# Layer-1 retention in a two-layer hybrid backbone: token tiles copied by ScalarE ahead of the first scores, and VectorE in program order up to them

## The chip, the cores and the metric

The kernel runs on one core of a Trainium2 chip. The engines of a core run their own instruction streams and wait for each other through semaphores: TensorE (PE, matmuls, reads SBUF and writes the PSUM banks), VectorE (DVE), ScalarE (ACT), GpSimd (POOL), and SyncE (SP), which here only issues transfers. The metric is device time in microseconds of one execution, the median of three runs.

## The reference

Two layers over 256 latent tokens and 256 context tokens of width 1024. Layer 0 is windowed attention beside a gated linear recurrence. Layer 1, the last, is a retention mixer, and each layer ends with a SwiGLU network. The part that matters here is the start of layer 1 (cut, names kept):

```python
def modulate(h, shift, scale):
    return h * (1.0 + scale) + shift

h_lat = modulate(rms_norm(x, norm_g[layer, 0]), m_lat[0], m_lat[1])
h_ctx = modulate(rms_norm(ctx, norm_g[layer, 0]), m_ctx[0], m_ctx[1])

def odd_mixer(h_ctx, h_lat, w_in, w_out, cos, sin, need_ctx):   # 4 heads, dk 256, dv 512
    p = split_parts(h_lat @ w_in, ODD_PARTS)                      # q, k, v, gate
    pc = project_parts(h_ctx, w_in, ODD_PARTS, ['k', 'v'])        # last layer: context gives k, v only
    q_l = apply_rope(q of p); k_l = apply_rope(k of p) * k_scale
    # forward and backward retention: scores (q k^T) times a decay matrix, times v, over latent and context
    y_lat = gated_head_norm(o_fw + flip(o_bw), p['g']).astype(dt) @ w_out
```

## The kernel before, in words

**Precision.** Every fp32 operand of a large matmul is split into two parts of type fp32r: a high half, which ScalarE makes by a rounding copy, and a rest (value minus high half), which VectorE makes. A product is three matmuls: high x high, rest x high, high x rest (L341, L342, L343; L338 and L339 do it in two where the operand's parts lie side by side). Tiles `hh` and `hl` are high half and rest of the normed input, `whi` and `wlo` those of a weight piece, `u` are working tiles.

**Weights.** All weights stream in one sequence of pieces of 128 x 1024. `ensure` loads a piece into one of three `raw` buffers (SP issues the transfer), ScalarE makes `whi` (L268), VectorE `wlo` (L269), each with four buffers. A raw buffer is free for the next transfer when its `wlo` is made; a `whi` buffer when TensorE has read it.

**Order.** The kernel is written against a scheduler that chooses each engine's instruction order from the dependences; inside `tc.manual_schedule` an engine keeps the order in which the program calls it. Side work is written as generators in lanes ('b', 'c', 't', 'r'). `work` counts matmul columns and now and then takes one step of each lane; `drain(lane)` runs a lane to its end. `modt` sets how many such steps lie between two rows of the modulation matrix (L233).

**Start of layer 1.** The norm of the latent stream runs ahead of its statistics: `first_group` multiplies the unnormed, scaled latent input (258 columns: 256 tokens and the shift) and afterwards `fix` (L458, L459) scales the four results by the norm's factor. For the context stream, and for the latent input of the later groups, `Norm.finish` works block by block (eight blocks of 128 rows): `scaled` (L478, VectorE) puts the scaled block into a tile, `shifted` makes its high half with the shift added (L484, ScalarE) and its rest (L485, VectorE). Lane 'b' holds the latent stream's finish, lane 'c' the context's. After the group comes the context's part of the keys (`pc`), then:

- `rope` (L1071 to L1073) rotates keys and query on VectorE, and `split` (L435 on ScalarE, L436 on VectorE) makes their halves;
- `tok_lane` multiplies the normed input by an identity (L1086, L1087), which lays it out by tokens: four token blocks times two halves of the width, eight tiles in PSUM, each split into `htok`;
- `ret_gate` projects the gate (two column blocks), `ret_scores` makes the scores (two banks of 128 x 512), multiplies them by the decay matrix (L1143) and splits them;
- `ret_values` sums the token tiles with the scores (`sums`), and projects the sums with the value weights (L338, L339), eight steps of 2.85 us each or so at TensorE.

PSUM has two pools of four banks: `mm`, which `first_group` and the projections take, and `ax`, which the context's keys, the token tiles, the scores and the sums take. A bank is taken again when the last reader of its tile is done.

Of the kernel before, what the change touches and what calls it, by code (L numbers as in the profile page):

```python
# [16 lines left out]
P = 128  # L17
# [15 lines left out]
N_PIECE = N_BLOCKS // PIECE  # L33
LOOK = 2
LN = 2
MODT = [4.6, 5.5, 4, 4]
QD = 3
FA = 2
PES = [3]
# [29 lines left out]
def hybrid_kernel(ctx, tc, xT, wst, mw0, mwT, small, cbc, cst, imask, dmat, out, order):  # L69
# [19 lines left out]
    def u(shape=(P, NT), dt=F32):  # L89
        return up.tile(list(shape), dt, tag="u", name=nm("u"))  # L90
# [305 lines left out]
    def first_group(src, cols, nl, hs, n_ctx):  # L396

        ps = [mmb() for _ in cols]
        ws = {}
        for i in K8:  # L400
            for j in range(len(cols)):
                ws[i, j] = take(src, i, cols[j])
                mm3(ps[j][:, 0:LW], ws[i, j], nl.p[i], i == 0, i == KD - 1)
        drain('b')
        lat = [nl.fix(p) for p in ps]
        drain('c')
        ctx = []
        for j in range(n_ctx):
            pc = (axb if j < FA else mmb)()
            for i in K8:  # L410
                mm3(pc[:, 0:L], ws[i, j], cut(hs[i], CTX), i == 0, i == KD - 1)
            ctx.append(pc[:, 0:L])
        return lat, ctx
# [646 lines left out]
    ffn(0, hs, (0, 1), n1, nl)  # L1060
    HS = [(a[:], b[:]) for a, b in hh]

    modt[0] = MODT[2]
    O_K, O_Q, O_V, O_G = 0, 2, 4, 8
    y1 = [None] * 16

# [8 lines left out]
    identr = cp.tile([P, P], F32R, tag="idr", name="idr")  # L1075
    A.activation(identr[:], ident, AF.Copy)
    htok = [[None, None] for _ in range(4)]

    def tok_lane():

        for st in range(4):
            for half in range(2):
                ps = axb((P, 4, P))
                for i in range(4):
                    hi, lo = cut(HS[half * 4 + i], slice(st * P, (st + 1) * P))
                    T.matmul(ps[:, i, :], hi, identr[:], start=True, stop=False)  # L1086
                    T.matmul(ps[:, i, :], lo, identr[:], start=False, stop=True)  # L1087
                th, tl = u((P, 4, P), F32R), u((P, 4, P), F32R)
                split(ps[:], th[:], tl[:])
                htok[st][half] = (th, tl)  # L1090
                yield

    def ret_kq(hd):
        c = 12 * hd
        if hd == 0:
            lat, kc = first_group('oin', [c + O_K, c + O_K + 1, c + O_Q, c + O_Q + 1], n1[0], HS, 2)
            for t, b in lat:
                A.activation(t, t, AF.Identity, bias=b)
            (k0, _), (k1, _), (q0, _), (q1, _) = lat
            start('t', tok_lane())  # L1100
        else:
            pk = group('oin', [c + O_K, c + O_K + 1], K8, HS, kouter=False)
            k0, k1 = pk[0][:, LAT], pk[1][:, LAT]
            kc = [pk[0][:, CTX], pk[1][:, CTX]]
        kf = [u(), u()]
        kk = []
        rope([kf[0][:, LAT], kf[1][:, LAT]], k0, k1)
        for i in range(2):
            A.activation(kf[i][:, CTX], kc[i], AF.Copy)
            hi, lo = u(dt=F32R), u(dt=F32R)  # L1110
            split(kf[i][:], hi[:], lo[:])
            kk.append((hi[:], lo[:]))
        if hd:
            pq = group('oin', [c + O_Q, c + O_Q + 1], K8, HS, sls=(LAT,), kouter=False)
            q0, q1 = pq[0][:, LAT], pq[1][:, LAT]
        qf = u((P, 2, L))
        rope([qf[:, 0, :], qf[:, 1, :]], q0, q1)
        qhi, qlo = u((P, 2, L), F32R), u((P, 2, L), F32R)
        split(qf[:], qhi[:], qlo[:])
        return kk, (qhi, qlo)  # L1120
# [81 lines left out]
                split(yf[hd][d2][:, i, :], t[:, 0], t[:, 1])  # L1202
                y1[hd * 4 + d2 * 2 + i] = parts2(t)

    for hd in range(4):
        kk, qq = ret_kq(hd)
        g = [ret_gate(hd, 0)]
        pp = ret_scores(hd, kk, qq)
        drain('r')
        if hd == 3:  # L1210
            y_split(0)
# [141 lines left out]
```

## Time and profile before

| | |
|---|---|
| time, median of 3 runs (range) | 1143.65 us (1143.5 to 1143.72) |
| time of the profiled execution | 1143.34 us |
| its span, first to last instruction | 1141.6 us |
| mean granted TensorE clock, share of full | 0.997 |
| TensorE busy, share of the span | 97% |
| VectorE busy | 70% |
| ScalarE busy | 50% |
| HBM traffic, mean over the span | 156 GB/s |

The profiled execution stands for the runs: its own time lies 0.31 us below their median, and 1.7 us of it lie outside the span. A busy share is a mean over stages; what one stage waits for is read from that stage.

### The profile page before, as it was taken

The page shows a single profiled execution, that of the slowest core. Times are in us where ns is not written, and L with a number is a line of the kernel's source. Part 1 is how long each engine was busy: PE and PEld are TensorE (multiplying, and loading weights), DVE is VectorE, ACT ScalarE, POOL GpSimd, SP SyncE. Part 2 cuts the span into 40 slices and gives each one's busy share as a digit, 9 for nine tenths or more (in the row PEclk, how much of TensorE's full clock was granted, in tenths as well). Part 3 has the DMA queues.
Part 4 walks back from the last instruction along what each step waited for, and adds up shares of the span by engine and source line. Part 5 has one row for each costly group of instructions (what it writes and reads, how often), then busy time and mean ns, then how long its engine had stood idle before and what let it go on. Part 6 is the DMA issues. An engine that isn't in the chain of part 4 may idle for free.

```text
span 1141.6 us, 17475 instructions
## 1 busy us (share of the span) xinstructions
PE 1110.1 (97%) x6762; PEld 956.6 (84%) x6762; DVE 797.9 (70%) x1479; ACT 567.6 (50%) x996; POOL 20.8 (2%) x46
## 2 busy tenths in 40 slices
PE   3999999999999999999999998999999999999998
PEld 1777877888998888988888898998989888888887
DVE  3877698999798557347884668474747588767764
ACT  5676676674753222122322466454545557654651
POOL 0012000000000000000000000000000000000000
PEclk9999999999999999999999999999999999999999
DMA  9987222326337446247983323344434365655663
GB/s 328 350 237 185 93 60 71 106 80 196 101 108 243 139 156 203 75 131 228 322 311 114 106 80 116 118 122 126 132 111 146 94 192 160 200 183 184 189 188 105
DMA packets 56115, 182.37 MB, mean 160 GB/s; under 512 B 6368, under 2 KB 9824, under 8 KB 55904
## 3 DMA queue, kind: packets, MB, share of 16 engines
q1 hardware_dynamic: 53648, 176.45, 48.3%
q0 software_dynamic: 2240, 4.72, 1.7%
q8 instruction: 53, 0.87, 0.3%
q14 instruction: 30, 0.25, 0.1%
q10 hardware_dynamic: 144, 0.08, 0.0%
HBM read 177.56 MB, written 1.05 MB: 156 GB/s over the span
## 4 chain that ended last, share of the span: by engine, by line
PE 87%; DVE 8%; ACT 2%; DMA 1%; issue 1%; DVEq 0%; ACTq 0%; SPq 0%
PE mm L343 17%; PE mm L341 17%; PE mm L342 17%; PE mm L338 13%; PE mm L339 6%; PE ax L342 2%; PE ax L341 2%; PE ax L343 2%; DVE wlo L269 2%; PE ax L338 1%; PE ax L175 1%; PE ax L675 1%; PE ax L694 1%; DVE u L478 1%; DMA raw<-in_wst_dram 1%
## 5 line engine op out<-in xcount | busy, mean ns | idle before, releaser
L268 ACT ACTIVATE whi<-raw 128x1024 fp32r<-128x1024 f32 x230 | 243.2, 1058 | 366.7 <-PE mm L342 177.1
L269 DVE TENSOR_TENSOR wlo<-raw,whi 128x1024 fp32r<-128x1024 f32 x230 | 280.8, 1223 | 134.5 <-ACT whi L268 133.5
L341 PE MATMUL mm<-hh,whi 128*128 128x512 f32 (+1 forms) x752 | 271.9, 362 | 0.9 <-ACT whi L268 0.9
L342 PE MATMUL mm<-hl,whi 128*128 128x512 f32 (+1 forms) x752 | 271.9, 362 | 0.1
L343 PE MATMUL mm<-hh,wlo 128*128 128x512 f32 (+1 forms) x752 | 271.1, 361 | 0.6 <-DVE wlo L269 0.6
L343 PEld LDWEIGHTS mm<-hh,wlo 128*128 128x128 f32 x752 | 143.0, 190 | 21.6 <-DVE wlo L269 0.8
L341 PEld LDWEIGHTS mm<-hh,whi 128*128 128x128 f32 x752 | 142.8, 190 | 21.5 <-ACT whi L268 0.9
L342 PEld LDWEIGHTS mm<-hl,whi 128*128 128x128 f32 x752 | 143.2, 191 | 20.2 <-DVE hl L485 0.3
L338 PE MATMUL mm<-u,whi 128*128 128x512 f32 x368 | 131.9, 399 | 2.3 <-DVE x L502 1.7
L342 PE MATMUL mm<-u,whi 128*128 128x512 f32 (+2 forms) x336 | 114.5, 341 | 0.0
L343 PE MATMUL mm<-u,wlo 128*128 128x512 f32 (+2 forms) x336 | 114.3, 341 | 0.0
L341 PE MATMUL mm<-u,whi 128*128 128x512 f32 (+2 forms) x336 | 114.1, 341 | 0.0
L338 PE MATMUL mm<-hh,whi 128*128 128x512 f32 x320 | 111.9, 395 | 1.7 <-DVE u L459 1.2
L339 PE MATMUL mm<-u,wlo 128*128 128x256 f32 x368 | 103.0, 280 | 0.0
L233 DVE CUSTOM_DVE_ANT_0 mr<-mr,cb 128x1024 f32<-128x1024 f32 x72 | 87.1, 1223 | 14.4 <-DMA mr<-in_mwT_dram 13.8
L339 PE MATMUL mm<-hh,wlo 128*128 128x256 f32 x320 | 89.5, 280 | 0.0
L338 PEld LDWEIGHTS mm<-u,whi 128*128 128x128 f32 x368 | 69.1, 188 | 19.0 <-PE mm L339 1.4
L338 PEld LDWEIGHTS mm<-hh,whi 128*128 128x128 f32 x320 | 59.9, 187 | 15.9 <-ACT whi L268 1.3
L341 PEld LDWEIGHTS mm<-u,whi 128*128 128x128 f32 x336 | 63.6, 189 | 7.2
L343 PEld LDWEIGHTS mm<-u,wlo 128*128 128x128 f32 x336 | 63.6, 189 | 7.1
L342 PEld LDWEIGHTS mm<-u,whi 128*128 128x128 f32 x336 | 63.7, 190 | 7.0
L339 PEld LDWEIGHTS mm<-u,wlo 128*128 128x128 f32 x368 | 69.5, 189 | 0.1
(238 smaller groups left out, 1666.8 us busy)
## 6 DMA issues: line engine op xcount, KB each, us to landing
raw<-in_wst_dram SPq DMA_DIRECT2D x230, 512.0 KB, 3.7
mr<-in_mwT_dram SPq DMA_DIRECT2D x80, 512.0 KB, 4.5
u<-in_mw_dram SPq DMA_DIRECT2D x16, 256.0 KB, 5.2
u<-u POOLq DMA_DIRECT2D x20, 128.0 KB, 6.3
u<-in_dmat_dram POOLq DMA_DIRECT2D x8, 256.0 KB, 3.1
raw<-in_mw_dram SPq DMA_DIRECT2D x6, 256.0 KB, 5.2
mr<-in_mw_dram SPq DMA_DIRECT2D x6, 256.0 KB, 5.2
x<-in_xT_dram SPq DMA_DIRECT2D x8, 128.0 KB, 3.3
```

The lines of the kernel that those rows point to most:

```text
L175: T.matmul(ps[32 * g:32 * g + 32, :], cT[:, k, :], mws[nt * 8 + k], start=(k < 4), stop=(k >= 4), skip_group_check=True)
L233: V.tensor_tensor_reduce(o, mr[:], cb[:, s, :], 1.0, 0.0, ALU.mult, ALU.add, mvec(l, s, ch, k))
L268: A.activation(hi[:], src[:], AF.Copy)
L269: V.tensor_tensor(lo[:], src[:], hi[:].bitcast(F32), ALU.subtract)
L338: T.matmul(o, w[0], a[2], start=first, stop=False, skip_group_check=True)
L339: anchor[0] = T.matmul(o[:, 0:L], w[1], a[0], start=False, stop=last, skip_group_check=True)
L341: T.matmul(o, w[0], a[0], start=first, stop=False, skip_group_check=shared)
L342: T.matmul(o, w[0], a[1], start=False, stop=False, skip_group_check=shared)
L343: anchor[0] = T.matmul(o, w[1], a[0], start=False, stop=last, skip_group_check=shared)
L478: V.scalar_tensor_tensor(t, xs(k, self.s), gsv[:, self.l, self.j, self.s, k:k + 1], self.r, ALU.mult, ALU.mult)
L675: T.transpose(tp[:, i, :], p[:, i * P:(i + 1) * P], ident)
L694: T.matmul(o[64 * j:64 * j + 64, col:col + P], vtok[:, kk, 64 * j:64 * j + 64], pts[3 * j + w][:, blk, :], start=(n == 0), stop=last, skip ...
```

## The change

Five edits, all at the start of layer 1:

1. In the first head, `ret_head` runs up to the scores inside `tc.manual_schedule` for VectorE alone: there VectorE's instructions stand in the order in which the program calls them. The other engines are scheduled as before.
2. In `first_group` of layer 1's first norm, lane 'c' (context) is drained ahead of the fix and lane 'b' (latent) behind it, where it was the other way round.
3. `tok_lane` goes over the halves outside and the token blocks inside. Six of the eight tiles are copied to SBUF by ScalarE (two stay in PSUM). The splits of all eight come after the last copy, as later steps of the lane.
4. `ret_head` runs the lane until all eight tiles are laid out before it calls `ret_scores`.
5. The steps between modulation rows: 10^9 up to the scores, then 2.9, where it was 4.

```diff
-MODT = [4.6, 5.5, 4, 4]
+MODT = [4.6, 5.5, 2.9, 4]
@@ first_group
-        drain('b')
-        lat = [nl.fix(p) for p in ps]
-        drain('c')
+        if nl.j == 0:
+            drain('c')
+            lat = [nl.fix(p) for p in ps]
+            drain('b')
+        else:
+            drain('b')
+            lat = [nl.fix(p) for p in ps]
+            drain('c')
@@
-    modt[0] = MODT[2]
+    modt[0] = 10 ** 9
@@
+    tokt = []
     def tok_lane():
-        for st in range(4):
-            for half in range(2):
+        for half in range(2):
+            for st in range(4):
                 ps = axb((P, 4, P))
                 for i in range(4):
                     hi, lo = cut(HS[half * 4 + i], slice(st * P, (st + 1) * P))
                     T.matmul(ps[:, i, :], hi, identr[:], start=True, stop=False)
                     T.matmul(ps[:, i, :], lo, identr[:], start=False, stop=True)
-                th, tl = u((P, 4, P), F32R), u((P, 4, P), F32R)
-                split(ps[:], th[:], tl[:])
-                htok[st][half] = (th, tl)
+                if half == 0 or st < 2:
+                    t = u((P, 4, P))
+                    A.activation(t[:], ps[:], AF.Copy)
+                else:
+                    t = ps
+                tokt.append((st, half, t))
                 yield
+        for st, half, t in tokt:
+            th, tl = u((P, 4, P), F32R), u((P, 4, P), F32R)
+            split(t[:], th[:], tl[:])
+            htok[st][half] = (th, tl)
+            yield
@@ ret_kq
-            start('t', tok_lane())
+            push('t', tok_lane())
@@
-    for hd in range(4):
+    def ret_head(hd):
         kk, qq = ret_kq(hd)
         g = [ret_gate(hd, 0)]
-        pp = ret_scores(hd, kk, qq)
+        while hd == 0 and len(tokt) < 8:
+            next(lanes['t'][0])
+        return g, ret_scores(hd, kk, qq)
+
+    for hd in range(4):
+        if hd == 0:
+            with tc.manual_schedule(engines={V.engine}):
+                g, pp = ret_head(hd)
+            modt[0], tickn[0] = MODT[2], 0
+        else:
+            g, pp = ret_head(hd)
         drain('r')
```

In the changed file the lines of the helpers move by five or so: L478, L484 and L485 become L483, L489 and L490; `fix` L463 and L464; `split` L440 and L441; the multiply by the decay matrix L1158. The new copies are L1097. The sequence of transfers on SP is the same in both programs, and so is the order of every engine ahead of and behind this place.

How the instructions stand on VectorE from the context's first block on, before (the numbers behind the names are those of the tiles):

```order
L478 SCALAR_TENSOR_TENSOR u_6273<-u_94,gsv,u_6269 128x256
L478 SCALAR_TENSOR_TENSOR u_6277<-u_94,gsv,u_6269 128x256
L478 SCALAR_TENSOR_TENSOR u_6281<-u_95,gsv,u_6269 128x256
L485 SCALAR_TENSOR_TENSOR hl_3423<-u_6273,modv,hh_3422 128x256
L485 SCALAR_TENSOR_TENSOR hl_3425<-u_6277,modv,hh_3424 128x256
L485 SCALAR_TENSOR_TENSOR hl_3427<-u_6281,modv,hh_3426 128x256
L478 SCALAR_TENSOR_TENSOR u_6285<-u_95,gsv,u_6269 128x256
L478 SCALAR_TENSOR_TENSOR u_6289<-u_96,gsv,u_6269 128x256
L478 SCALAR_TENSOR_TENSOR u_6293<-u_96,gsv,u_6269 128x256
L485 SCALAR_TENSOR_TENSOR hl_3429<-u_6285,modv,hh_3428 128x256
```

And in the changed program, from the seventh of the context's eight blocks over the latent ones on (12 rows; behind them stand the rest of `u_6387`, one more latent pair and then the fix):

```order
L483 SCALAR_TENSOR_TENSOR u_6296<-u_97,gsv,u_6268 128x256
L490 SCALAR_TENSOR_TENSOR hl_3435<-u_6296,modv,hh_3434 128x256
L483 SCALAR_TENSOR_TENSOR u_6300<-u_97,gsv,u_6268 128x256
L490 SCALAR_TENSOR_TENSOR hl_3437<-u_6300,modv,hh_3436 128x256
L269 TENSOR_TENSOR wlo_6316<-raw_6313,whi_6315 128x1024
L483 SCALAR_TENSOR_TENSOR u_6331<-x_90,gsv,u_6149 128x256
L490 SCALAR_TENSOR_TENSOR hl_3431<-u_6331,modv,hh_3430 128x256
L269 TENSOR_TENSOR wlo_6350<-raw_6347,whi_6349 128x1024
L483 SCALAR_TENSOR_TENSOR u_6359<-x_91,gsv,u_6149 128x256
L490 SCALAR_TENSOR_TENSOR hl_3433<-u_6359,modv,hh_3432 128x256
L269 TENSOR_TENSOR wlo_6384<-raw_6381,whi_6383 128x1024
L483 SCALAR_TENSOR_TENSOR u_6387<-x_92,gsv,u_6149 128x256
```

What moved: a block's rest stands directly behind the scaling that it is made from, where two scalings of other blocks stood between; and three weight rests stand between the latent blocks.

VectorE again, around the query's rotation, before:

```order
L1072 TENSOR_TENSOR u_6543<-u_6441,con 128x256
L269 TENSOR_TENSOR wlo_6728<-raw_6725,whi_6727 128x1024
L1073 TENSOR_TENSOR u_6542<-u_6543 128x256
L1071 TENSOR_TENSOR u_6547<-u_6445,con 128x256
L1072 TENSOR_TENSOR u_6547<-u_6441,con 128x256
L1073 TENSOR_TENSOR u_6542<-u_6547 128x256
L436 TENSOR_TENSOR u_6552<-u_6542,u_6551 128x512
L269 TENSOR_TENSOR wlo_6775<-raw_6772,whi_6774 128x1024
L436 TENSOR_TENSOR u_6579<-ax_6569,u_6578 128x512
```

And in the changed program:

```order
L1078 TENSOR_TENSOR u_6509<-u_6514 128x256
L441 TENSOR_TENSOR u_6519<-u_6509,u_6518 128x512
L269 TENSOR_TENSOR wlo_6527<-raw_6524,whi_6526 128x1024
L269 TENSOR_TENSOR wlo_6579<-raw_6576,whi_6578 128x1024
L269 TENSOR_TENSOR wlo_6723<-raw_6720,whi_6722 128x1024
L269 TENSOR_TENSOR wlo_6757<-raw_6754,whi_6756 128x1024
L1158 TENSOR_TENSOR u_6688<-ax_6675,u_6671 128x512
L441 TENSOR_TENSOR u_6691<-u_6688,u_6690 128x512
L441 TENSOR_TENSOR u_6696<-u_6542,u_6695 128x512
```

What moved: the weight rests that lay between the rotations follow the rest of the query (`u_6519`) in one run of four, ahead of the multiply of the first scores.

ScalarE from the query's high half on, before (`u_6551`):

```order
L435 ACTIVATE u_6551<-u_6542 128x512
L268 ACTIVATE whi_6774<-raw_6772 128x1024
L435 ACTIVATE u_6578<-ax_6569 128x512
L435 ACTIVATE u_6612<-ax_6603 128x512
L435 ACTIVATE u_6652<-ax_6643 128x512
L1127 ACT_TABLE_LOAD
L1127 ACTIVATE u_6665<-mm_6555 128x256
```

And in the changed program, where it is `u_6518`; `ax_6631` and `ax_6642` are the fifth and sixth token tile, and their banks become those of the two score tiles:

```order
L440 ACTIVATE u_6518<-u_6509 128x512
L1097 ACTIVATE u_6542<-ax_6533 128x512
L1097 ACTIVATE u_6571<-ax_6562 128x512
L1097 ACTIVATE u_6606<-ax_6597 128x512
L1142 ACT_TABLE_LOAD
L1142 ACTIVATE u_6617<-mm_6522 128x256
L1142 ACTIVATE u_6617<-mm_6523 128x256
L1097 ACTIVATE u_6629<-ax_6620 128x512
L268 ACTIVATE whi_6756<-raw_6754 128x1024
L1097 ACTIVATE u_6640<-ax_6631 128x512
L1097 ACTIVATE u_6651<-ax_6642 128x512
L440 ACTIVATE u_6690<-u_6688 128x512
```

What moved: the token copies stand behind the query's high half, the last three of them behind the table load and the gate's two activations, and the last two also behind the high half of a weight piece.

## Rows read from the trace of the kernel before

**Rows 1.** The page's first part: busy time in us, share of the span and instructions of each engine.

```profile
PE 1110.1 (97%) x6762; PEld 956.6 (84%) x6762; DVE 797.9 (70%) x1479; ACT 567.6 (50%) x996; POOL 20.8 (2%) x46
```

**Rows 2.** The table of stretches: the stretch in us, its length, busy time and instructions of each engine, the granted TensorE clock as a share of full (PEclk), the share of the DMA engines, GB/s.

```profile
697.00:701.00 4.00, 0.79 (x7) 0.59 (x6) 3.27 (x7) 1.26 (x2) 0.00 (x0) 1.00 0.40 145
701.00:705.00 4.00, 4.00 (x24) 4.00 (x22) 3.71 (x6) 3.71 (x7) 0.00 (x0) 0.57 0.37 100
```

**Rows 3.** TensorE's timeline: start in us, duration, line, operation, tiles, shapes; in brackets the idle time before the row and what ended it.

```profile
687.18 0.22 PE L1086 MATMUL ax<-idr,hh 128*128 128x128 f32 x1
...
687.36 0.27 PE L1086 MATMUL ax<-idr,hh 128*128 128x128 f32 x1
687.47 0.27 PE L1087 MATMUL ax<-idr,hl 128*128 128x128 f32 x1
...
696.81 0.28 PE L341 MATMUL mm<-hh,whi 128*128 128x256 f32 x1
696.93 0.28 PE L342 MATMUL mm<-hl,whi 128*128 128x256 f32 x1
700.42 0.39 PE L341 MATMUL ax<-u,u 128*128 128x256 f32 x1 [3.21 <-ACT u L435]
...
703.09 0.41 PE L341 MATMUL ax<-u,u 128*128 128x256 f32 x1
703.30 0.41 PE L342 MATMUL ax<-u,u 128*128 128x256 f32 x1
...
717.15 0.50 PE L338 MATMUL mm<-u,whi 128*128 128x512 f32 x1
```

**Rows 4.** VectorE's timeline, the same columns (x3 at the end of a row: three equal instructions in a run, with their time in all).

```profile
671.43 1.22 DVE L269 TENSOR_TENSOR wlo<-raw,whi 128x1024 fp32r<-128x1024 f32 x1
...
673.30 0.48 DVE L478 SCALAR_TENSOR_TENSOR u<-x,gsv,u 128x256 f32<-128x256 f32 x1
674.36 0.48 DVE L485 SCALAR_TENSOR_TENSOR hl<-u,modv,hh 128x256 fp32r<-128x256 f32 x1 [0.58 <-ACT hh L484]
676.45 0.48 DVE L478 SCALAR_TENSOR_TENSOR u<-u,gsv,u 128x256 f32<-128x256 f32 x1 [1.61 <-ACT u L475]
...
684.77 0.48 DVE L478 SCALAR_TENSOR_TENSOR u<-x,gsv,u 128x256 f32<-128x256 f32 x1
685.16 0.48 DVE L485 SCALAR_TENSOR_TENSOR hl<-u,modv,hh 128x256 fp32r<-128x256 f32 x1
685.56 0.15 DVE L458 COPY s<-mm 128x1 f32<-128x1 f32 x1
...
686.35 2.35 DVE L269 TENSOR_TENSOR wlo<-raw,whi 128x1024 fp32r<-128x1024 f32 x2
...
691.54 0.42 DVE L1071 TENSOR_TENSOR u<-u,con 128x256 f32<-128x256 f32 x1
...
700.40 0.69 DVE L436 TENSOR_TENSOR u<-u,u 128x512 fp32r<-128x512 f32 x1 [0.69 <-ACT u L435]
...
702.49 1.88 DVE L436 TENSOR_TENSOR u<-ax,u 128x512 fp32r<-128x512 f32 x3
704.29 0.68 DVE L1143 TENSOR_TENSOR u<-ax,u 128x512 f32<-128x512 f32 x1
```

**Rows 5.** ScalarE's timeline, the same columns.

```profile
673.81 0.51 ACT L484 ACTIVATE hh<-u,modv 128x256 fp32r<-128x256 f32 x1 [0.82 <-DVE u L478]
...
685.11 2.01 ACT L268 ACTIVATE whi<-raw 128x1024 fp32r<-128x1024 f32 x2
...
699.74 0.63 ACT L435 ACTIVATE u<-u 128x512 fp32r<-128x512 f32 x1 [3.08 <-DVE u L1073]
...
701.22 1.55 ACT L435 ACTIVATE u<-ax 128x512 fp32r<-128x512 f32 x3
702.79 1.28 ACT L1127 ACT_TABLE_LOAD   x1
704.08 0.66 ACT L1127 ACTIVATE u<-mm 128x256 f32<-128x256 f32 x2
705.00 0.63 ACT L435 ACTIVATE u<-u 128x512 fp32r<-128x512 f32 x1 [0.26 <-DVE u L1143]
```

**Rows 6.** Groups of instructions by line between 685 and 717.2 us: count, busy us, mean ns of one, then the idle time before them and what ended it; VectorE's weight rests.

```profile
L269 DVE TENSOR_TENSOR wlo<-raw,whi 128x1024 fp32r<-128x1024 f32 x8 | 9.7, 1222 | 3.4 <-ACT whi L268 3.4
```

**Rows 7.** The page's sixth part: transfers of the weight pieces, count, KB each, median us from issue to landing.

```profile
raw<-in_wst_dram SPq DMA_DIRECT2D x230, 512.0 KB, 3.7
```

**Rows 8.** The table of stretches for line L233 alone (the rows of the modulation matrix): the stretch, its length, VectorE's busy time and count, granted clock, DMA share, GB/s.

```profile
600.00:650.00 50.00, 1.42 (x4) 1.00 0.35 106
650.00:760.00 110.00, 0.00 (x0) 0.98 0.36 110
760.00:1141.00 381.00, 0.00 (x0) 1.00 0.50 154
```

**Rows 9.** TensorE's two next longest waits after the start of the program, and the table of stretches (columns as in rows 2) around them.

```profile
925.50 0.47 PE L338 MATMUL mm<-u,whi 128*128 128x512 f32 x1 [0.85 <-DVE x L502]
961.70 0.47 PE L338 MATMUL mm<-hh,whi 128*128 128x512 f32 x1 [1.16 <-DVE u L459]
920.00:930.00 10.00, 9.15 (x53) 7.78 (x52) 8.13 (x17) 5.45 (x13) 0.00 (x0) 1.00 0.59 199
956.00:966.00 10.00, 8.84 (x63) 8.13 (x62) 10.00 (x25) 6.78 (x12) 0.00 (x0) 1.00 0.44 136
```

## The prediction, on record before the changed kernel ran

> **What bounds the kernel now.** I read the page's table of engines first. TensorE is busy 97% of the span [rows 1], so a change elsewhere matters only where it makes TensorE wait or lets it stop waiting. The second view was the table of stretches around the first scores of layer 1: between 697 and 701 us TensorE is busy 0.79 of 4 us, and in the next 4 us the granted clock is 0.57 of full, so part of them ran at 1.2 GHz instead of 2.4 [rows 2]. The third was TensorE's timeline [rows 3]. The reader is to see the wait of 3.21 us at 700.42, released by ScalarE's L435, and that after it the matmuls start 0.21 us apart instead of 0.12. The wait with its gap (696.93 to 700.42 less one step) costs 3.37 us, and some 15 steps at 0.213 instead of 0.12 another 1.4. So this place holds 4.8 us that a better order could give back, and no more.
>
> What released it is on the vector engine: it is at work nearly without a gap from 676.45 to the high half of the query at 699.74 on ScalarE and its rest at 700.40 [rows 4, 5].
>
> **The change, part by part.** *The interleaving numbers* (2.9 for 4, and 10^9 until the scores) cost nothing: they pace the modulation rows (L233), and the last of these run before 650 us; there are none afterwards [rows 8].
>
> *VectorE's program order.* The two DVE pieces of the section on the change show it. Each row block of the norm is a pair: L478 scales (VectorE), L484 makes the high half (ScalarE), L485 the rest (VectorE). The scheduler had put the scalings ahead and the rests behind, so ScalarE worked under cover of the next scaling; two instructions then cost 0.80 us (684.77 to 685.16 to 685.56). Written as in the program, L485 of a block stands directly behind its L478, with nothing between to cover ScalarE. The trace has one such pair: L478 at 673.30, L484 at 673.81, L485 at 674.36 with 0.58 idle [rows 4, 5]. That is 1.06, and 0.40 for L485 itself: 1.46 a pair, 0.66 of it idle. Twelve pairs stand so between the second norm statistics and the fix: 17.5 us, where before the first eleven took 685.56 - 676.45 = 9.1.
>
> The rest follows in VectorE's order up to the fix (L458, L459):
> - Start: before, the first context scaling is at 676.45. One weight rest (671.43) leaves the place ahead of the sum that the statistics wait for, at most 1.13 us; I take 0.9, so 675.55.
> - ScalarE makes a weight piece's high half between the fourth and the fifth context pair, and it can't start until TensorE has read the buffer that it reuses, which waits for that pair: +0.95 (half of the two in 2.01) [rows 5].
> - Three weight rests stand among the last four pairs, 1.13 each by their spacing [rows 4]: 3.4.
> - Sum: 675.55 + 17.5 + 0.95 + 3.4 = 697.4, against 685.56.
>
> Behind the fix stands TensorE. The four accumulators of the first group hold all four `mm` banks, so the gate's first matmul waits until the first of them is read: 697.4 + 0.5 (two fixes take 0.79) = 697.9. All token groups now stand behind that matmul. Before, this work began at 687.18 [rows 3]. So TensorE reaches the same point **10.7 us late**, and it stands idle for some 5 us before it.
>
> *Token tiles ahead of the scores, by ScalarE's copies.* Six copies are new on ScalarE, about 0.5 each (three such rows in 1.55 [rows 5]); their price is in the chain below. From there to the first projection matmul (L338, 717.15) the work is the same in both: 64 token matmuls at 0.112, 96 gate matmuls, 24 of scores and 24 of sums at 0.12, 24.4 us. Before it took 29.97: 24.4, the 4.8 above, and 0.8 of small gaps. What it takes after, I work out along VectorE and ScalarE:
> - Fix, two in 0.79 (685.56 to 686.35), four in 1.6: 699.0. Rotations and splits up to the query's high half: 8.20 before (691.54 to 699.74), less two weight rests that stand outside now, 5.9: 704.9. High half 0.63, rest queued behind it: VectorE is free at 706.2.
> - Only then comes the weight rest `wlo_6527`, whose raw buffer the piece `raw_6754` needs: 707.4. The load takes 3.7 [rows 7]: 711.1. ScalarE's high half of that piece stands ahead of the token copies 6640 and 6651 (ACT piece of the change): 712.1, and the copy 0.6. The first scores need the bank of that copy: **712.7**. TensorE's own work, 48 gate and 64 token matmuls, ends at 710.8, so it waits 1.9. This wait is new.
> - Scores, multiply (0.69), high half (0.63), rest, one token rest, the second multiply: 12 matmuls at 0.12 and 0.28 give 714.3, then 716.9 and 718.3 at the start of the last score rest. From there VectorE has eight splits at 0.60 (1.88 for three) and two weight rests: 4.8 + 2.3, plus two waits for ScalarE of about 0.3 (3.4 over eight such rows [rows 6]): 726.0. The first sum's rest, 0.45, stands behind all the token splits: L338 at **726.5**, where TensorE alone could have had it at 724.
>
> So the stretch is 28.6 instead of 29.97 long, and it begins 10.7 late: +9.3 us at L338. From there the rows are the same in both programs and TensorE is the bound.
>
> *The clock.* After 3.21 us idle it fell to half for a time that cost 1.4. It will be low after the 5 us before the gate, but there the wait for the copies (1.9) covers 1.4. After the last wait of some 2.3 us it may fall or not: the trace has no wait between 1.16 us, where the clock stayed full, and 3.21 [rows 3, 9]. I take half, 0.7. The Trainium skill's page "TensorE: Matmul & The Clock Gate" (A second HAM failure mode: psum-queue depth-cycling) says that frequent short idle spells between groups of matmuls are enough to make the clock swing between half and full. By it the clock could fall before the gate already and again behind it: that is the last rival below, up to 1162.6. No stretch of this trace has such a series of idle spells to show it.
>
> **Sum.** +9.3 + 0.7 = +10.0 on the profiled execution's own 1143.34 (its span of 1141.6 and 1.7 around it): 1153.3. The median of the runs shown is 0.3 above that execution: **1153.6 us**. Bounds: without either later wait, the gate's lateness stays and the stretch is 25.2: 697.9 + 25.2 - 717.15 = +5.95, 1149.6; with 1.4 for the clock in full at both waits, +12.1, 1155.7.
>
> **Rivals.**
> - *Faster: the pairs overlap and the banks come free.* VectorE does lose work ahead of the query: three weight rests and one token split, 3 x 1.13 + 0.60 = 4.0. For it speaks that the same instructions took 0.80 a pair before. Then the gate starts 12 x 0.66 = 7.9 earlier, at 690.0, and with no later wait L338 comes at 715.2: -1.95, **1141.7**. It decides at the idle time per pair: 1.95 / 12 = 0.16 us is all that may be left. Against it: VectorE took nothing else in the 0.58 idle, and the rows leave nothing between. 4%.
> - *No difference* (within 0.2%, about 2.3 us, which is what a measurement of this kernel can tell from no change): the pairs overlap, but the waits at the scores stay; 690.0 + 28.6 - 717.15 = +1.45, **1145.1**. 4%.
> - *Half the loss*: lateness as forecast, but copies and splits come in time: **1149.6**. The token copies are short (three in 1.55), but two stand behind a table load of 1.28 and one behind the load of a piece [rows 5]. 9%.
> - *The clock stays at half from the gate to L338.* The mechanism would be TensorE's short idle times between context pairs, then 5 us idle, then waits. 48 gate matmuls at 0.213 bring TensorE to the scores at 715.2 instead of 712.7; the 72 matmuls and the last sums behind add up to 6.5: +9 in the worst case, **1158 to 1162.6**. Against it: the one fall in the middle of this trace ended by 704.4, with TensorE at work [rows 3]. 9%.
>
> My forecast has the other 74%, and its own range is 1151 to 1157. **The range** that holds eight in ten takes in the bounds and most of the case "half the loss": 1149.3 to 1158. Left out are the two cases with overlap (8%), most of the clock's (7%), and tails. Faster 0.04, same 0.04, slower 0.92.
>
> **What would show it.** In the profile after: L490 rows with an idle time of about 0.6 each, released by ScalarE's L489, twelve times; the fix (L463) near 697 instead of 685.6; one wait of TensorE of about 5 us at the gate's first matmul, released by VectorE's L464; a wait of 1 to 2 us at the first scores, released by an L1097 copy; the first L338 near 726; from there on the timeline of before, shifted. A fix before 691 would show the serial pairs wrong. A first L338 near 723 would show the two later waits wrong. A granted clock of 0.5 in several stretches from 690 on would show the clock's price too small.

## The result

| | median, us | range, runs |
|---|---|---|
| before | 1143.68 | 1143.5 to 1145.28, 4 |
| changed | 1156.34 | 1155.44 to 1158.81, 4 |

The ratio is 1.0112, with a 95% interval of 1.01 to 1.0124: **12.7 us slower**. The forecast was 1153.6 us, with a range of 1149.3 to 1158, so the time lies inside it, 2.7 us above the forecast. The profiled execution took 1155.55 us, of which the span is 1153.8, against 1143.34 and 1141.6 before.

The page's table of engines (compare [rows 1]: busy us, share of the span, instructions):

```profile
PE 1114.6 (97%) x6762; PEld 959.0 (83%) x6762; DVE 799.0 (69%) x1479; ACT 571.6 (50%) x1002; POOL 20.9 (2%) x46
```

TensorE has 4.5 us more of busy time, with the same matmuls, and 7.7 us more without work. The table of stretches says where (compare [rows 2]; the columns are the same):

```profile
674.00:687.00 13.00, 12.10 (x87) 10.58 (x85) 6.65 (x15) 6.98 (x12) 1.12 (x2) 1.00 0.14 42
...
689.00:693.00 4.00, 3.80 (x19) 3.80 (x20) 2.85 (x6) 1.29 (x3) 0.00 (x0) 0.60 0.46 133
...
697.00:701.00 4.00, 2.90 (x13) 2.93 (x14) 3.86 (x15) 2.91 (x8) 0.00 (x0) 0.50 0.05 20
701.00:705.00 4.00, 4.00 (x27) 4.00 (x26) 3.77 (x9) 0.63 (x1) 0.00 (x0) 0.70 0.00 0
705.00:709.00 4.00, 4.00 (x36) 4.00 (x35) 2.18 (x4) 3.44 (x6) 0.00 (x0) 1.00 0.00 0
...
729.00:733.00 4.00, 3.90 (x25) 3.58 (x26) 0.71 (x3) 0.39 (x1) 0.00 (x0) 1.00 0.07 25
```

Until 687 us the clock is full. Then TensorE waits, and the clock is 0.60, 0.50 and 0.70 of full in the next three stretches shown. From 701 to 705 TensorE is busy throughout, and the table counts 27 matmuls; in the next 4 us, at full clock, 36. The last row is behind the last wait, and there the clock is full.

TensorE's timeline at its waits (compare [rows 3]):

```profile
689.20 0.79 PE L343 MATMUL mm<-u,wlo 128*128 128x258 f32 x4 [2.09 <-DVE wlo L269]
...
698.10 0.55 PE L341 MATMUL mm<-hh,whi 128*128 128x256 f32 x1 [4.25 <-DVE u L464]
698.45 0.41 PE L342 MATMUL mm<-hl,whi 128*128 128x256 f32 x1
698.67 0.41 PE L343 MATMUL mm<-hh,wlo 128*128 128x256 f32 x1
...
715.18 0.39 PE L341 MATMUL ax<-u,u 128*128 128x256 f32 x1 [1.58 <-ACT u L1097]
...
729.10 0.50 PE L338 MATMUL mm<-u,whi 128*128 128x512 f32 x1 [2.15 <-DVE u L441]
```

The wait of 3.21 at the first scores is gone. In its place stand four: 2.09 for a weight rest, 4.25 at the gate for the fix, 1.58 at the first scores for a token copy, 2.15 at the first projection. Behind the wait at the gate the matmuls start 0.22 apart. The first L338 is at 729.10 instead of 717.15, 11.95 us later, which is the whole difference of the spans (12.2) but 0.25.

VectorE's rests L490 and weight rests between the context's first scaling and the fix, as groups (count, busy us, mean ns; then the idle time ahead of them and what ended it):

```profile
L490 DVE SCALAR_TENSOR_TENSOR hl<-u,modv,hh 128x256 fp32r<-128x256 f32 x12 | 5.8, 485 | 7.9 <-ACT hh L489 7.9
...
L269 DVE TENSOR_TENSOR wlo<-raw,whi 128x1024 fp32r<-128x1024 f32 x3 | 3.7, 1218 | 0.0
```

And VectorE's timeline (compare [rows 4]):

```profile
676.61 0.48 DVE L490 SCALAR_TENSOR_TENSOR hl<-u,modv,hh 128x256 fp32r<-128x256 f32 x1 [0.58 <-ACT hh L489]
677.01 0.48 DVE L483 SCALAR_TENSOR_TENSOR u<-u,gsv,u 128x256 f32<-128x256 f32 x1
678.07 0.48 DVE L490 SCALAR_TENSOR_TENSOR hl<-u,modv,hh 128x256 fp32r<-128x256 f32 x1 [0.58 <-ACT hh L489]
...
697.47 0.15 DVE L463 COPY s<-mm 128x1 f32<-128x1 f32 x1
...
706.94 0.69 DVE L441 TENSOR_TENSOR u<-u,u 128x512 fp32r<-128x512 f32 x1 [1.82 <-ACT u L440]
707.55 3.49 DVE L269 TENSOR_TENSOR wlo<-raw,whi 128x1024 fp32r<-128x1024 f32 x3
714.67 1.23 DVE L269 TENSOR_TENSOR wlo<-raw,whi 128x1024 fp32r<-128x1024 f32 x1 [3.63 <-ACT whi L268]
716.92 0.69 DVE L1158 TENSOR_TENSOR u<-ax,u 128x512 f32<-128x512 f32 x1 [1.02 <-PE ax L343]
```

Twelve pairs, 7.9 us of idle time ahead of their rests, all of it ended by ScalarE's high halves. The three rows at 676.61 to 678.07 show one period: 1.46 us. Before, the fix (first L458) stood at 685.56; here it is at 697.47.

### The profile page after: what moved, and what is told of

It reads as the page before. It is cut to its first block, busy times and chain, and to the rows that moved or that the text cites. A ratio compares the mean times of both kernels' runs of the same rounds, so it can differ in the third digit from the quotient of the medians.

```text
span 1153.8 us, 17482 instructions
## 1 busy us (share of the span) xinstructions
PE 1114.6 (97%) x6762; PEld 959.0 (83%) x6762; DVE 799.0 (69%) x1479; ACT 571.6 (50%) x1002; POOL 20.9 (2%) x46
## 4 chain that ended last, share of the span: by engine, by line
PE 87%; DVE 8%; ACT 3%; DMA 2%; issue 1%; DVEq 0%; ACTq 0%; SPq 0%
PE mm L341 16%; PE mm L343 16%; PE mm L342 16%; PE mm L338 13%; PE mm L339 6%; PE ax L341 2%; PE ax L342 2%; PE ax L343 2%; DMA raw<-in_wst_dram 1%; DVE wlo L269 1%; PE ax L338 1%; PE ax L175 1%; ACT whi L268 1%; PE ax L680 1%; PE ax L699 1%
## 5 line engine op out<-in xcount | busy, mean ns | idle before, releaser
L268 ACT ACTIVATE whi<-raw 128x1024 fp32r<-128x1024 f32 x230 | 243.4, 1059 | 370.2 <-PE mm L342 177.8
L338 PE MATMUL mm<-u,whi 128*128 128x512 f32 x368 | 132.2, 400 | 4.6 <-DVE u L441 2.7
L338 PE MATMUL mm<-hh,whi 128*128 128x512 f32 x320 | 112.1, 396 | 1.3 <-DVE u L464 1.2
L233 DVE CUSTOM_DVE_ANT_0 mr<-mr,cb 128x1024 f32<-128x1024 f32 x72 | 87.2, 1223 | 14.7 <-DMA mr<-in_mwT_dram 14.4
L338 PEld LDWEIGHTS mm<-u,whi 128*128 128x128 f32 x368 | 69.1, 188 | 21.5 <-DVE u L441 3.2
L338 PEld LDWEIGHTS mm<-hh,whi 128*128 128x128 f32 x320 | 60.0, 188 | 16.0 <-ACT whi L268 1.3
```

What stands on the lines that cost most here:

```text
L233: V.tensor_tensor_reduce(o, mr[:], cb[:, s, :], 1.0, 0.0, ALU.mult, ALU.add, mvec(l, s, ch, k))
L268: A.activation(hi[:], src[:], AF.Copy)
L338: T.matmul(o, w[0], a[2], start=first, stop=False, skip_group_check=True)
```

## The experiments

Eight kernels ran, four and four beside runs of the kernel before (1143.95 us, 1141.7 to 1145.41, 11 runs, for the first four; 1144.02, 1142.12 to 1146.1, 21 runs, for the others). The table puts them side by side. "Fix" is the start of the first L463 (L458 in before), "stretch" the time from there to the first projection matmul, both from one profile; this takes out that, ahead of the stretch already, a profile lies up to 1.1 us off the one of before. Differences below 1 us between starts in two profiles mean nothing, then.

| kernel | median us | ratio to before (interval) | fix | stretch |
|---|---|---|---|---|
| before | 1143.7 to 1144.0 | 1 | 685.56 | 31.59 |
| changed | 1156.34 | 1.0112 (1.01 to 1.0124) | 697.47 | 31.63 |
| e1, no program order | 1148.81 | 1.0044 (1.0031 to 1.0057) | 685.86 | 36.37 |
| e2, program order alone | 1151.37 | 1.0065 (1.0052 to 1.0077) | 698.27 | 26.09 |
| e3, scalings one ahead | 1149.54 | 1.0049 (1.0032 to 1.0066) | 690.59 | 30.55 |
| e4, TensorE kept busy | 1154.80 | 1.0096 (1.0083 to 1.0109) | 698.30 | 29.36 |
| e5, rests behind the query | 1141.42 | 0.9977 (0.9968 to 0.9986) | 686.67 | 28.12 |
| e6, numbers back | 1172.05 | 1.0254 (1.0239 to 1.0269) | 702.79 | 39.83 |
| e7, no loop | 1153.22 | 1.0083 (1.0069 to 1.0097) | 697.69 | 29.01 |
| e8, copies alone | 1141.88 | 0.9983 (0.9975 to 0.9992) | 685.86 | 30.26 |

### e1: without VectorE's program order

```diff
-            with tc.manual_schedule(engines={V.engine}):
-                g, pp = ret_head(hd)
+            g, pp = ret_head(hd)
```

> The change without VectorE's program order: the token copies, the loop ahead of the scores and the interleaving numbers stay, VectorE is scheduled as before. Theory (the serial pairs on VectorE are the loss): the fix is back near 685.6 and TensorE has no wait at the gate; about 1145 us (1143 to 1147), with a wait of 2 to 2.5 at the later token tiles or at the first L338, since six copies and eight splits are still squeezed between the fix and the sums. Rival (the token copies ahead of the scores are the loss): 1152 or more. Rival (clock): no series of stretches at half clock is left, so what the clock costs falls away with the gate's wait; same number as the theory, told apart by the granted clock.

Measured: 1148.81. The fix is back at 685.86 and the wait at the gate is gone, as the theory says. But the time is above its range of 1143 to 1147 and below the 1152 of the rival on the copies, and the rival on the clock is wrong: what the clock costs does not fall away with the wait at the gate. TensorE's waits, and the table of stretches:

```profile
700.29 0.43 PE L1093 MATMUL ax<-idr,hh 128*128 128x128 f32 x1 [2.28 <-ACT u L1097]
...
722.23 0.50 PE L338 MATMUL mm<-u,whi 128*128 128x512 f32 x1 [2.23 <-DVE u L441]
```

```profile
697.00:701.00 4.00, 1.72 (x13) 1.52 (x11) 3.75 (x8) 2.02 (x5) 0.00 (x0) 0.92 0.58 175
701.00:705.00 4.00, 4.00 (x21) 4.00 (x20) 0.00 (x0) 3.62 (x7) 0.00 (x0) 0.50 0.40 131
705.00:709.00 4.00, 4.00 (x20) 4.00 (x21) 0.00 (x0) 0.00 (x0) 0.00 (x0) 0.50 0.00 0
709.00:713.00 4.00, 4.00 (x29) 4.00 (x29) 2.27 (x4) 1.15 (x2) 0.00 (x0) 0.80 0.00 0
```

A wait of 2.28 for the bank of a token copy, and behind it a clock of 0.50 from 701 to 709 with TensorE busy all the time. In these 8 us the table counts 41 matmuls; for the 4 us from 701 in the kernel before, themselves partly at half clock, it has 24 [rows 2].

### e2: the program order without the token edits

```diff
-    modt[0] = MODT[2]
+    modt[0] = 10 ** 9
@@
-    for hd in range(4):
+    def ret_head(hd):
         kk, qq = ret_kq(hd)
         g = [ret_gate(hd, 0)]
-        pp = ret_scores(hd, kk, qq)
+        return g, ret_scores(hd, kk, qq)
+
+    for hd in range(4):
+        if hd == 0:
+            with tc.manual_schedule(engines={V.engine}):
+                g, pp = ret_head(hd)
+            modt[0], tickn[0] = MODT[2], 0
+        else:
+            g, pp = ret_head(hd)
```

> The kernel before with VectorE's program order up to the scores and the interleaving numbers, but the token lane and its splits as before. Theory (serial pairs): the fix near 697.5 and TensorE's wait at the gate as in the changed kernel; the new waits at the scores and at the first L338 are not there or under 1 us each; 1150 to 1153 us, that is two thirds of the loss or more. Rival (copies): within 0.3% of before, 1143 to 1147.

Measured: 1151.37, inside the theory's range. TensorE's wait at the gate, the only one of over 0.4 us from there on, and its first projection matmul, which has none:

```profile
698.90 0.36 PE L341 MATMUL mm<-hh,whi 128*128 128x256 f32 x1 [3.34 <-DVE u L459]
...
724.36 0.50 PE L338 MATMUL mm<-u,whi 128*128 128x512 f32 x1
```

e1 and e2 split the change: the token edits alone cost 1148.81 - 1143.95 = 4.9 us, the order alone 7.4. Their sum, 12.3, is the change's 12.7 within what these runs tell. That does not show that the two act apart from each other: the loop ahead of the scores, which is one of the token edits, costs 3.1 with the order (e7) and 6.9 without it (e8 against e1). The order's 7.4 is less than the 12.7 us by which its fix is late (some 0.7 of them were there ahead of this place in its profile), since the wait of 3.21 and its half clock fall away: the stretch is 26.09 instead of 31.59.

### e3: one scaling ahead

```diff
                 t = u()[:, 0:L]
                 self.scaled(k, t)
-                self.shifted(k, t)
+                if self.l == 1 and self.j == 0:
+                    if k:
+                        self.shifted(k - 1, prev)
+                    prev = t
+                else:
+                    self.shifted(k, t)
+            if self.l == 1 and self.j == 0:
+                self.shifted(KD - 1, prev)
```

> The changed kernel with one line moved in the norm: the scaling of block k+1 is called ahead of the rest of block k, so that VectorE's program order itself covers ScalarE. Theory (serial pairs): idle time ahead of the rests falls from 0.58 to under 0.1 each, the fix comes near 690 instead of 697.5, TensorE's wait at the gate falls from 4.4 to under 3, the waits at the scores (1.9) and at L338 (2.4) stay: 7.7 us less than the changed kernel, 1148.5 (1146.5 to 1149.5). Rival (waits behind absorb it): 1154 or more.

Measured: 1149.54 (1146.29 to 1151.36, 6 runs), 6.8 less than the changed kernel and 0.04 above the range that was given. VectorE's rests as a group, and TensorE's waits:

```profile
L490 DVE SCALAR_TENSOR_TENSOR hl<-u,modv,hh 128x256 fp32r<-128x256 f32 x13 | 6.2, 484 | 0.6 <-ACT hh L489 0.6
```

```profile
691.22 0.36 PE L341 MATMUL mm<-hh,whi 128*128 128x256 f32 x1 [2.95 <-DVE u L464]
...
707.21 0.39 PE L341 MATMUL ax<-u,u 128*128 128x256 f32 x1 [1.35 <-ACT u L1104]
...
721.14 0.50 PE L338 MATMUL mm<-u,whi 128*128 128x512 f32 x1 [2.15 <-DVE u L441]
```

The idle time ahead of thirteen rests is 0.6 in all, and the fix is at 690.59. From the context's first scaling to the fix it takes 14.23 us here, 21.92 in the changed kernel and 9.11 before. So the idle time in the pairs is the cause of 7.7 us of the late fix: the order stays fixed, the same three weight rests stand in it, and only what lies between the two instructions of a pair differs. Of the 5.1 us that are left, 3.4 are these weight rests. One thing behind the fix went otherwise than in the changed kernel: the last wait is as long (2.15), but the clock fell behind it:

```profile
721.00:725.00 4.00, 3.86 (x18) 3.64 (x19) 0.42 (x2) 0.00 (x0) 0.00 (x0) 0.66 0.06 20
```

0.66 here; the same wait in the changed kernel left it at 1.00.

### e4: TensorE kept busy ahead of the gate

```diff
             ctx.append(pc[:, 0:L])
+        if nl.l == 1 and nl.j == 0:
+            with tc.issue_after(anchor[0].ins):
+                for _ in range(30):
+                    T.matmul(pc[:, L:2 * L], identr[:], hs[0][0][:, CTX],
+                             start=True, stop=True, skip_group_check=True)
         return lat, ctx
```

> The changed kernel with 30 matmuls of 256 columns that compute nothing, written to the unused half of a context bank between the context's keys and the gate: TensorE is busy until about 697.2 instead of idle from 693.6 to 698.1. If the half clock behind that wait is on the path (the gate's 48 matmuls at 0.213, a weight's high half that waits for them and stands ahead of the query's high half on ScalarE): the gate runs at 0.12, that high half starts near 703 instead of 705.3, the query's high half near 705.1 instead of 706.3, and the time falls by 1.2 us, to 1155.1. If the overshoot comes from the piece's load alone: no difference, 1156.3. If the clock falls anyway: no difference, with the granted clock at half behind the gate.

Measured: 1154.80, 1.5 less than the changed kernel; its four runs (1153.72 to 1155.06) all lie below the four of that kernel (1155.44 to 1158.81). The table of stretches at the gate and behind the last wait, ScalarE's weight half L268 and query half L444 (L440 in the changed kernel), and the first projection matmul:

```profile
697.00:701.00 4.00, 3.59 (x31) 3.42 (x30) 3.33 (x13) 3.05 (x8) 0.00 (x0) 1.00 0.28 108
701.00:705.00 4.00, 4.00 (x37) 4.00 (x36) 3.77 (x10) 2.40 (x4) 0.00 (x0) 1.00 0.02 4
...
729.00:733.00 4.00, 4.00 (x19) 3.81 (x19) 0.42 (x1) 0.38 (x1) 0.00 (x0) 0.57 0.00 0
```

```profile
703.75 1.06 ACT L268 ACTIVATE whi<-raw 128x1024 fp32r<-128x1024 f32 x1 [0.78 <-PE mm L342]
705.99 0.63 ACT L444 ACTIVATE u<-u 128x512 fp32r<-128x512 f32 x1 [1.18 <-DVE u L1082]
```

```profile
727.66 0.50 PE L338 MATMUL mm<-u,whi 128*128 128x512 f32 x1 [2.15 <-DVE u L445]
```

The clock at the gate is full, the weight's half no longer holds back the query's, and the stretch is 29.36, 2.3 less than in the changed kernel. About half of the 2.3 is the query's high half: it starts 7.69 us behind the fix instead of 8.82. The other half is the load of the next piece, which took 3.58 here and 4.73 there, and nothing ties that to the clock. Part is given back: behind the last wait, again 2.15, the clock is 0.57, where in the changed kernel it was full. So the half clock's way through ScalarE is shown by the rows, at 1.1 us; how the 1.5 us of the medians divide between it and the load is not.

### e6: the interleaving numbers of before

```diff
-MODT = [4.6, 5.5, 2.9, 4]
+MODT = [4.6, 5.5, 4, 4]
@@
-    modt[0] = 10 ** 9
+    modt[0] = MODT[2]
@@
-            modt[0], tickn[0] = MODT[2], 0
```

> The changed kernel with the interleaving numbers as in the kernel before (4 throughout). Theory (VectorE's program order holds for whatever is called inside it): 27 of the modulation rows, which the scheduler had put ahead of 650 us, are called inside the block or behind its first instructions and now stand between the latent blocks and the sums, at 1.2 us each (two instructions of 0.6); 15 of them ahead of the first scores' multiply. The time is 1156.3 + 20 to 32, 1176 to 1188, with L233 rows on VectorE between 690 and 760 us. Rival (the numbers cost and save nothing, as the prediction's sentence on them could be read): 1156.3.

Measured: 1172.05, 15.7 more than the changed kernel and 4 below the theory's range. The modulation rows between 690 and 760 us as a group, and TensorE's wait at the gate:

```profile
L233 DVE CUSTOM_DVE_ANT_0 mr<-mr,cb 128x1024 f32<-128x1024 f32 x26 | 31.3, 1219 | 4.3 <-DMA mr<-in_mwT_dram 4.3
```

```profile
703.42 0.55 PE L341 MATMUL mm<-hh,whi 128*128 128x256 f32 x1 [9.10 <-DVE u L464]
```

Before and after the change not one such row lies here [rows 8]. A row is one instruction of 1.22 and a read of 0.08, not two of 0.6. The time rose by half of the 31 us. The rows that stand where VectorE would have been idle cost nothing, which the range given had not taken off; on the other side TensorE's waits are longer (9.10 here, 4.09 at the first L338), and the mean granted clock is 0.985 instead of 0.994. How much of the 15.7 is the clock was not told apart.

### e7: no loop ahead of the scores

```diff
-        while hd == 0 and len(tokt) < 8:
-            next(lanes['t'][0])
```

> The changed kernel without the loop that lays out all eight token tiles ahead of the scores. Theory (the wait of 1.9 at the first scores is for the copies' banks): that wait is gone, the wait at the gate (4.4) and the one at L338 (2.4) stay; 1.5 to 2 less than the changed kernel, 1154.5 us. Rival (the scores wait for the query itself): the wait stays with another releaser, 1156.3.

Measured: 1153.22, 3.1 less than the changed kernel, more than the theory gave. TensorE's waits from the gate on are two:

```profile
698.32 0.55 PE L341 MATMUL mm<-hh,whi 128*128 128x256 f32 x1 [4.26 <-DVE u L464]
...
726.70 0.50 PE L338 MATMUL mm<-u,whi 128*128 128x512 f32 x1 [0.77 <-DVE u L441]
```

The wait at the scores is gone, so it was for the banks of the copies. The last wait is 0.77 instead of 2.15 as well, which the theory had left as it was.

### e8: the copies alone

The kernel before with edits 2, 3 and 5 of the change: no program order on VectorE, no loop.

> The kernel before with the token lane's new shape (copies by ScalarE, splits behind the last tile) and nothing else that moves an instruction: VectorE is scheduled and the loop ahead of the scores is left out. Theory (token splits leave VectorE's work ahead of the query, 0.6, and the loop is what makes the banks late): TensorE's wait at the scores falls from 3.2 to about 2, a wait of about 1 comes at L338; 1142.5 to 1145 by whether the clock falls. If the scheduled version with the loop (1148.8) is slow by the copies themselves and not by the loop: 1147 or more.

Measured: 1141.88, 2.1 less than before, and a little below the range. TensorE waits 1.86 at the scores and 0.39 at L338:

```profile
699.79 0.39 PE L341 MATMUL ax<-u,u 128*128 128x256 f32 x1 [1.86 <-ACT u L440]
...
716.12 0.50 PE L338 MATMUL mm<-u,whi 128*128 128x512 f32 x1 [0.39 <-DVE u L441]
```

So copies by ScalarE cost nothing by themselves, with VectorE scheduled. What costs in e1 is the loop, which puts all eight tiles ahead of the scores: 1148.81 against 1141.88, with VectorE's order left to the scheduler in both.

### e5: the weight rests behind the query

```diff
     def ensure(p):
@@
-            V.tensor_tensor(lo[:], src[:], hi[:].bitcast(F32), ALU.subtract)
+            behind = tc.issue_after(qrest[1]) if qrest and q == qrest[0] else nullcontext()
+            with behind:
+                V.tensor_tensor(lo[:], src[:], hi[:].bitcast(F32), ALU.subtract)
@@ ret_kq                     (split returns its VectorE instruction)
-        split(qf[:], qhi[:], qlo[:])
+        rest = split(qf[:], qhi[:], qlo[:])
+        if hd == 0:
+            qrest[:] = [len(pieces), rest.ins]
```

> The kernel before with one edge of order: the first weight rest that is called after the query's rotation is issued on VectorE behind the query's rest; the scheduler then puts three weight rests (3 x 1.13 = 3.4 us) behind the query that lay ahead of it. Theory (in the kernel before, only VectorE's work ahead of the query kept TensorE waiting): TensorE's wait of 3.21 at 700.42 falls under 0.5, and with it the half clock behind it (1.4); 4.3 to 4.8 less, 1139.4 us (1138.8 to 1141). Rival (a weight rest that comes 3 us later makes TensorE wait at the gate or at the sums, or holds back the next piece's load): 1142.5 or more, with waits released by L269 or L268.

Measured: 1141.42, 2.6 less than before: faster than both kernels, a little above the theory's range and below the rival's 1142.5. TensorE's waits at the first scores, and the stretches around them:

```profile
698.29 0.38 PE L346 MATMUL ax<-u,u 128*128 128x256 f32 x1 [0.47 <-ACT u L440]
...
699.02 0.39 PE L347 MATMUL ax<-u,u 128*128 128x256 f32 x1 [0.34 <-DVE u L441]
```

```profile
697.00:701.00 4.00, 3.03 (x21) 2.43 (x21) 3.27 (x6) 3.37 (x5) 0.00 (x0) 1.00 0.03 6
701.00:705.00 4.00, 4.00 (x36) 4.00 (x36) 3.83 (x6) 1.82 (x4) 0.00 (x0) 1.00 0.72 235
```

The wait of 3.21 is down to 0.47 and 0.34, no weight is late, and the clock stays full (36 matmuls in 4 us, against 24 in [rows 2]). The stretch is 3.5 us shorter than before, where the theory had 4.3 to 4.8 (3.4 of rests and the clock), and the medians differ by 2.6 only. The profiled execution (1142.00) is the slowest of the eleven: it reached the fix 1.11 later than the one of before, the first L338 2.36 earlier (714.79), and lost 1.0 again behind it. One profile of each kernel does not tell what of this is chance.

## Why the prediction was right, and where its sizes were off

**The serial pairs: right.** Ten of the twelve rests wait 0.58, and two wait longer (1.29 and 0.88), behind a weight's high half on ScalarE. A period is 1.46, as worked out. The start was forecast at 675.55 and is 675.55; from there to the fix 21.85 were forecast and 21.92 measured. That the fix itself, forecast at 697.4, stands at 697.47 is in part luck: in the profiles of e2, e4 and e7, with the same pairs ahead of it, it stands at 698.27, 698.30 and 697.69. e3 shows the cause, since covering the pairs brings the fix to 690.59.

**The gate: right.** 697.9 was forecast, 698.10 measured, released by VectorE's L464. TensorE's idle time ahead of it came in two parts, 2.09 and 4.25, where one of some 5 was forecast.

**The two later waits: right in place and releaser, and e7 shows what the first one is for.** 1.9 was forecast at the scores and 2.3 at L338; measured are 1.58 and 2.15, with the gaps ahead of them 1.7 and 2.3.

**The clock at the gate: mis-sized, and this is where the sum came out short.** L338 was 2.6 us later than forecast (729.10 against 726.5), and 2.5 of them had come together by the first scores (715.18 against 712.7); from there to L338 13.8 was forecast and 13.9 measured. The text says that the clock "will be low after the 5 us before the gate, but there the wait for the copies (1.9) covers 1.4". It was low as said, but the cost ran along ScalarE and not along TensorE. ScalarE's timeline and, behind it, the chain of work that ended last (start us, us, what) show it:

```profile
705.33 1.06 ACT L268 ACTIVATE whi<-raw 128x1024 fp32r<-128x1024 f32 x1 [3.20 <-PE mm L342]
706.29 0.61 ACT L440 ACTIVATE u<-u 128x512 fp32r<-128x512 f32 x1
```

```profile
707.55 1.23 DVE wlo L269
708.83 4.73 DMA raw<-in_wst_dram
713.59 1.06 ACT whi L268
714.64 0.49 ACT u L1097
```

The weight's high half (705.33) needs a buffer that the gate's matmuls have read, and at half clock they read it late. In ScalarE's order it stands ahead of the query's high half, which so starts at 706.3 instead of 704.9; VectorE is free late, the weight rest that frees the raw buffer (707.55) is late, and so the load, the copies and the scores. That is 1.4 of the 2.6 us, and some 1.1 of the 1.4 is this buffer: VectorE's last rotation row is over at 705.1. Another 1.0 is the load itself: 4.73 instead of 3.7. In e4, where the clock is full and that load took 3.58, the stretch is 29.36, against 29.1 in the forecast's sum (726.5 - 697.4): with both out of the way the sum holds. e3 had a load of 4.50, so what made it long is not settled. Of the 2.7 us by which the median lies above the forecast, then, 2.6 had come by L338; the 0.7 put down for the clock behind the last wait was not spent in this profile, and the median lies 0.8 above the profiled execution where 0.3 was taken.

**The clock behind the last wait: it can go either way, as was taken.** The same wait of 2.15 left the clock full in the changed kernel's profile and low in e3 and e4; one of 2.23 in e1 left it full. It may be one source of the spread of the changed kernel's runs, 1155.4 to 1158.8, if it falls in some executions and not in others: the mean granted clock is 0.994 in the two short ones and 0.991 and 0.993 in the long ones (1157.12 and 1158.81), which fits only in part. That was not tried.

**The rival "the clock stays at half from the gate to L338"** was given 9%. The clock was back by 705 (1.00 in the stretch from there), so it did not happen in the changed kernel. But the argument against it, that the one fall in the trace of before ended with TensorE at work after 4 us, does not carry over: in e1 the clock was 0.50 for 8 us of unbroken work. The Trainium skill's page "TensorE: Matmul & The Clock Gate" (A second HAM failure mode: psum-queue depth-cycling) says that frequent short idle spells between groups of matmuls made the clock swing in another kernel. Here TensorE's three idle spells between the context pairs (0.43, 0.20 and 0.20 us, from 682.7 to 686.1) left it at 1.00 in the stretch from 674 to 687. It fell behind some single waits, the shortest of them 1.86 (e8, 0.62 in the 4 us from 701), and not behind others (1.72 in e4, 2.15 in the changed kernel). So the trace bears out that waits can make it swing; that short ones are enough no run here shows.

**"The interleaving numbers cost nothing": true of the whole change, but not for the reason given.** The text read from [rows 8] that no modulation row is left after 650 us. They run that early because the scheduler puts them there; the program calls many of them at this place. Inside VectorE's program order they would have stayed here (e6, 15.7 us). The edit is what keeps the order from costing more than twice as much. The swap of the two drains, though, moves no instruction: with and without it the order of each engine is the same.

**The rivals without a loss** needed pairs that overlap; they did not. "Half the loss" needed copies and splits in time; e2, which leaves the token edits out, is close to it with 1151.37, against the 1149.6 that was worked out. Two sums of the prediction are off by 0.1 and 0.2 (714.4 for 714.3 behind the first scores, 72 matmuls at 0.093 more are 6.7 and not 6.5); neither changes the forecast by more.

## What to carry to other kernels

An engine's program order is an order for every instruction that is called inside it, with the helpers' and the side work's. Before fixing it, look for pairs that hand over to another engine and back, and write the next pair's first half ahead of the second half of this one. Here a wait at one place was better met by moving behind it the few instructions that the trace shows ahead of it (e5, one edge, 2.6 us less) than by fixing a whole stretch (12.7 more). And ask of each stretch of low clock who reads TensorE's progress: the cost came out on ScalarE, through a buffer that was read late.

## What was not expected of the hardware

- The clock stayed at 0.50 for at least 8 us with TensorE busy 4.00 of each 4.00 us (e1, 701 to 709), where in the kernel before it was back by 704.5, 4 us after the wait (0.57 in the 4 us from 701, [rows 2]).
- Equal waits of 2.15 us at the same instruction left the clock at 1.00 (changed), 0.66 (e3) and 0.57 (e4) in stretches of 4 us behind it.
- Loads of one and the same piece took 3.58 (e4), 3.63 (e7), 4.50 (e3) and 4.73 us (changed). In all four the next two loads are issued some 1.1 and 2.3 us behind it, so that overlap does not tell the short ones from the long ones.
